# The probabilities' transposes of a two-layer diffusion backbone, moved from a pair of PSUM banks to single banks

## The chip, the core and the metric

The kernel runs on one core of a Trainium2 chip. The core has a matrix engine (PE, whose weight loads are shown apart as PEld), a vector engine (DVE), a scalar engine (ACT), a third elementwise engine (POOL) and a queue that issues DMAs (SP). PE writes its results to PSUM, which this program uses as eight banks of 512 float32 columns on 128 partitions; ACT and DVE read them there. The metric is the device time of one execution in microseconds (us). Lower is better.

## The reference

Two layers run over 128 context tokens and 512 latent tokens of width 1024. Each layer normalises and modulates its input, projects it once, and feeds four parallel mixers: a short gated convolution, windowed attention with eight heads (GQA), neighbourhood attention with four heads (NA) and latent attention with four heads (MLA). The outputs are gated, merged and projected; then comes an MLP. The part that matters here is the softmax attention, which every attention mixer has in this form, cut:

```python
def dense_attention(q, k, v, scale, sink=None):
    ...
    def one_block(qi):
        s = jnp.einsum('nqkgd,nskd->nkgqs', qi, k).astype(jnp.float32) * scale
        p = softmax_sink(s, sink)
        return jnp.einsum('nkgqs,nskd->nqkgd', p.astype(v.dtype), v)
    ...
```

Values are float32. The kernel gets float32 accuracy out of faster matmuls by splitting each operand into a rounded part (hi) and a remainder (lo).

## The kernel before

A layer has three stages: the mixers (`mixers`), the merge of the branches and the MLP. In the merge and the MLP all eight banks are single ones. In the mixers, about 75 to 490 us and 1250 to 1690 us of the span, `psum(4, 2)` cuts them into four single banks (`bank`, tile name pr) and two pairs of two (`banks2`, tile name S2, shown as S). The change touches only the mixers.

There, `attend` goes over 80 blocks of each layer, one block a round: a head has four blocks of 128 latent queries and a short one of 128 context queries. The work of a block is spread over several rounds.

- `block_scores` (lines 503 to 508) takes a pair, computes scores on PE and their minimum on DVE (line 539 with a mask table, line 542 without). `block_exp` (line 548) takes the exponential on ACT from the pair to the tile p in SBUF; it is the last reader of the scores. `block_norm` divides on POOL (line 553). This runs AHEAD = 3 blocks before the block is used.
- `block_T` takes another pair and transposes p on PE, one 128x128 matmul for each chunk of 128 keys (line 562): four, five or six chunks for a latent block, one for a context block. One ACT cast writes the hi part to SBUF (line 566). `block_lo` subtracts it on DVE to get the lo part (line 569); it is the last reader of that pair.
- `pair_pv` (line 579) multiplies two blocks' transposed probabilities by the values into a single bank, read by ACT (line 583) and DVE (lines 592 to 602).
- `fill` puts other matmuls between these steps: the input projection and some of the gates, in halves of 24 matmuls (lines 226 to 228), each half in a single bank that ACT reads afterwards (lines 323, 324, 850, 902), and the small products of MLA (lines 1441 to 1454), whose keys ACT and DVE split (lines 240, 241).

PE's order is the order in which the code calls it. The other engines' orders are set by a scheduler at build time. A tile waits for its bank until the last reader of the tile that held it is done; which of the free banks a tile gets is decided at build time too.

Of the kernel before, what the change touches and what calls it, by code (L numbers as in the profile page):

```python
# [12 lines left out]
ALU = mybir.AluOpType  # L13
# [4 lines left out]
P = 128  # L18
# [58 lines left out]
def _r(ap):  # L77
    return ap.bitcast(F32)


class Net:
# [473 lines left out]
    def block_T(self, B):  # L555
        nc = self.nc
        if B["u"] == 0:
            B["pair"]["pt"] = self.at.tile([P, 2, 6, 256], F32R, name="pt", tag="pt", bufs=2)
        pt, p, nb = B["pair"]["pt"], B["p"], B["nb"]
        tp = self.banks2()  # L560
        for i, s in enumerate(B["pos"]):
            nc.tensor.transpose(tp[:, s * P:(s + 1) * P], p[:, i * P:(i + 1) * P], self.ident)  # L562
        src = tp[:, :nb * P].rearrange("p (c q) -> p c q", q=P)
        qs = slice(B["u"] * P, (B["u"] + 1) * P)
        B["hi"], B["lo"], B["src"] = pt[:, 0, 0:nb, qs], pt[:, 1, 0:nb, qs], src
        nc.scalar.copy(B["hi"], src)  # L566

    def block_lo(self, B):
        self.nc.vector.tensor_tensor(B["lo"], B["src"], _r(B["hi"]), ALU.subtract)  # L569

    def pair_pv(self, R):

# [1050 lines left out]
```

## Time and profile before

| | us |
|---|---|
| median of 3 runs | 2407.87 (2407.02 to 2413.71) |
| the profiled execution | 2411.14 |
| its span, from the first to the last instruction | 2409.3 |
| PE busy in the span | 2319.6 |
| DVE, ACT, POOL busy | 1392.7, 932.9, 415.0 |

An engine that waits shows a gap in the timeline, and the profile names the operation whose end let it go on (`<-`). For PE the table of waits adds such gaps up by its own line and by the releaser. The granted clock (PEclk) is the share of TensorE's full speed that it was given in a stretch; it has the two levels 1.0 (2.4 GHz) and 0.5 (1.2 GHz) here, and a mean between them is a mixture.

### The profile page before, as it was taken

The numbers are of one execution on the slowest core, as the hardware profiler recorded it, in microseconds if no ns is written. First come the engines' busy times: TensorE is split into PE (matmuls) and PEld (weight loads), VectorE is DVE, ScalarE is ACT, GpSimd is POOL, SyncE is SP. The second block draws the span as 40 slices with busy tenths as digits, with TensorE's granted clock in tenths as the row PEclk, the third lists the DMA queues.
The fourth block names the chain that finished last, engine by engine and source line by source line (L and its number), as shares of the span: only waits on it lengthen the run. The fifth ranks groups of instructions, "written<-read, shape, count | busy, mean of one in ns | idle before, by whom it ended". The sixth has DMA issues, their size and how long they took to land. (4 is left out here: it accounts for less than half of the span.)

```text
span 2409.3 us, 39780 instructions
## 1 busy us (share of the span) xinstructions
PE 2319.6 (96%) x15766; PEld 2258.7 (94%) x15766; DVE 1392.7 (58%) x2732; ACT 932.9 (39%) x1891; POOL 415.0 (17%) x496
## 2 busy tenths in 40 slices
PE   8998999899999999999999999999999999999998
PEld 4998889899999999999999999888999999999998
DVE  5765566556775787777576655655434554343433
ACT  5555555442224432322254555553322344231311
POOL 0322233202231000000023233322012300000001
PEclk9999999899999999999999999998999999999999
DMA  6331321154542344444331323220424312222222
GB/s 240 95 103 55 92 89 68 46 202 163 174 155 79 128 153 158 165 142 158 114 133 65 108 96 92 79 71 35 177 92 134 105 45 70 80 71 79 74 84 72
DMA packets 91371, 261.33 MB, mean 108 GB/s; under 512 B 10416, under 2 KB 29232, under 8 KB 89776
## 3 DMA queue, kind: packets, MB, share of 16 engines
q1 hardware_dynamic: 91184, 258.78, 31.8%
q8 instruction: 124, 2.03, 0.3%
q14 instruction: 63, 0.52, 0.1%
HBM read 231.31 MB, written 21.92 MB: 105 GB/s over the span
## 5 line engine op out<-in xcount | busy, mean ns | idle before, releaser
L226 PE MATMUL pr<-hhi,whiw 128*128 128x320 f32 (+1 forms) x2752 | 867.9, 315 | 2.9 <-ACT st L324 1.5
L228 PE MATMUL pr<-hhi,wlow 128*128 128x320 f32 (+1 forms) x2752 | 852.7, 310 | 3.0 <-DVE wlow L193 2.1
L227 PE MATMUL pr<-hlo,whiw 128*128 128x320 f32 (+1 forms) x2752 | 853.3, 310 | 0.0
L226 PEld LDWEIGHTS pr<-hhi,whiw 128*128 128x128 f32 (+1 forms) x2752 | 516.8, 188 | 5.7 <-ACT whiw L192 2.1
L228 PEld LDWEIGHTS pr<-hhi,wlow 128*128 128x128 f32 (+1 forms) x2752 | 515.8, 187 | 5.8 <-DVE wlow L193 3.5
L227 PEld LDWEIGHTS pr<-hlo,whiw 128*128 128x128 f32 (+1 forms) x2752 | 516.8, 188 | 3.6 <-DVE hlo L1249 2.5
L192 ACT CAST whiw<-raww 128x1024 fp32r<-128x1024 f32 (+2 forms) x170 | 173.5, 1021 | 299.8 <-PE pr L227 262.3
L226 PE MATMUL pr<-hh,whiw 128*128 128x320 f32 x832 | 257.1, 309 | 0.0
L228 PE MATMUL pr<-hh,wlow 128*128 128x320 f32 x832 | 256.9, 309 | 0.0
L227 PE MATMUL pr<-hl,whiw 128*128 128x320 f32 x832 | 256.9, 309 | 0.0
L193 DVE TENSOR_TENSOR wlow<-raww,whiw 128x1024 fp32r<-128x1024 f32 (+2 forms) x170 | 208.2, 1225 | 62.1 <-ACT whiw L192 61.6
L1002 DVE SCALAR_TENSOR_TENSOR x<-pr,mod,x 128x256 f32<-128x256 f32 x320 | 107.6, 379 | 188.4 <-PE pr L228 186.2
L1204 POOL TENSOR_TENSOR sqs<-sqs,sq 128x320 f32<-128x320 f32 x48 | 47.7, 993 | 972.1 <-ACT sq L1202 944.4
L553 POOL TENSOR_SCALAR p<-p,sm 128x512 f32<-128x512 f32 (+3 forms) x160 | 118.5, 741 | 440.6 <-DVE sm L552 416.0
L548 ACT ACTIVATE p<-S,sm 128x641 f32<-128x641 f32 (+6 forms) x160 | 111.9, 699 | 181.4 <-DVE sm L539 91.1
L975 POOL TENSOR_TENSOR acc<-acc,sg 128x320 f32<-128x320 f32 x96 | 100.2, 1058 | 340.6 <-DVE sg L974 340.5
L226 PEld LDWEIGHTS pr<-hh,whiw 128*128 128x128 f32 x832 | 156.4, 188 | 0.0
L228 PEld LDWEIGHTS pr<-hh,wlow 128*128 128x128 f32 x832 | 156.4, 188 | 0.0
L227 PEld LDWEIGHTS pr<-hl,whiw 128*128 128x128 f32 x832 | 156.4, 188 | 0.0
L569 DVE TENSOR_TENSOR pt<-S,pt 128x512 fp32r<-128x512 f32 (+3 forms) x160 | 112.1, 701 | 68.7 <-ACT pt L566 67.3
L276 DVE SCALAR_TENSOR_TENSOR junk<-wm,cb 128x1024 bf16<-128x1024 f32 x112 | 136.8, 1222 | 2.0
L190 POOL TENSOR_TENSOR wlow<-raww,whiw 128x512 fp32r<-128x512 f32 (+1 forms) x72 | 92.9, 1290 | 194.8 <-ACT whiw L189 183.1
(224 smaller groups left out, 3820.1 us busy)
## 6 DMA issues: line engine op xcount, KB each, us to landing
raww<-in_w SPq DMA_DIRECT2D x128, 512.0 KB, 3.5
wm<-in_wm SPq DMA_DIRECT2D x80, 512.0 KB, 3.5
raww<-in_wg SPq DMA_DIRECT2D x64, 512.0 KB, 3.7
raww<-in_wa SPq DMA_DIRECT2D x42, 512.0 KB, 3.5
gdram<-gt SPq DMA_DIRECT2D x28, 320.0 KB, 2.2
wm<-in_wm SPq DMA_DIRECT2D x8, 1024.0 KB, 14.5
raww<-in_wo SPq DMA_DIRECT2D x16, 512.0 KB, 3.4
kt<-kt SPq DMA_DIRECT2D x24, 224.0 KB, 4.6
```

Of the source, the lines that this page charges most:

```text
L190: e.tensor_tensor(lo[:, c], raw[:, c], _r(hi[:, c]), ALU.subtract)
L192: nc.scalar.copy(hi, raw)
L193: nc.vector.tensor_tensor(lo, raw, _r(hi), ALU.subtract)
L226: nc.tensor.matmul(out, lhsT=whi[:, kw, :], rhs=xhi[:, kx, sl], start=(i == 0), stop=False)
L227: nc.tensor.matmul(out, lhsT=whi[:, kw, :], rhs=xlo[:, kx, sl], start=False, stop=False)
L228: nc.tensor.matmul(out, lhsT=wlo[:, kw, :], rhs=xhi[:, kx, sl], start=False, stop=(i == n - 1))
L276: nc.vector.scalar_tensor_tensor(self.junk, raw, 1.0, self.cb[v], ALU.mult, ALU.mult, accum_out=self.mod[l]["mod"][:, v, i:i + 1])
L548: nc.scalar.activation(p[:, :B["n"]], B["sc"], AF.Exp, bias=sm[:, 0:1], scale=-1.0, accum_out=sm[:, 1:2])
L553: nc.gpsimd.tensor_scalar(p[:, :n], p[:, :n], sm[:, 1:2], 1.0, ALU.mult, ALU.mult)
L569: self.nc.vector.tensor_tensor(B["lo"], B["src"], _r(B["hi"]), ALU.subtract)
L975: nc.gpsimd.tensor_tensor(a, a, sg, ALU.add)
L1002: self.nc.vector.scalar_tensor_tensor(x[:, j, o + a:o + b], ps[:, a:b], m[:, v, g0 + j:g0 + j + 1], x[:, j, o + a:o + b], ALU.mult, ALU.add)
```

## The change

`block_T` no longer takes a pair. It goes over the chunks four at a time; each group of up to four takes a single bank, and has an ACT cast and a DVE subtraction of its own. A block of one or four chunks has one group as before; the 48 blocks of five chunks are split 4 + 1 and the 32 blocks of six chunks 4 + 2. The two pairs are left to the scores and to the transposes of the values in `v_pair`, three times a layer.

```diff
-        tp = self.banks2()
-        for i, s in enumerate(B["pos"]):
-            nc.tensor.transpose(tp[:, s * P:(s + 1) * P], p[:, i * P:(i + 1) * P], self.ident)
-        src = tp[:, :nb * P].rearrange("p (c q) -> p c q", q=P)
         qs = slice(B["u"] * P, (B["u"] + 1) * P)
-        B["hi"], B["lo"], B["src"] = pt[:, 0, 0:nb, qs], pt[:, 1, 0:nb, qs], src
-        nc.scalar.copy(B["hi"], src)
+        B["split"] = []
+
+        for c0 in range(0, nb, 4):
+            c1 = min(nb, c0 + 4)
+            tp = self.bank()
+            for i, s in enumerate(B["pos"]):
+                if c0 <= s < c1:
+                    nc.tensor.transpose(tp[:, (s - c0) * P:(s - c0 + 1) * P], p[:, i * P:(i + 1) * P], self.ident)
+            src = tp[:, :(c1 - c0) * P].rearrange("p (c q) -> p c q", q=P)
+            B["split"].append((pt[:, 0, c0:c1, qs], pt[:, 1, c0:c1, qs], src))
+            nc.scalar.copy(B["split"][-1][0], src)

     def block_lo(self, B):
-        self.nc.vector.tensor_tensor(B["lo"], B["src"], _r(B["hi"]), ALU.subtract)
+        for hi, lo, src in B["split"]:
+            self.nc.vector.tensor_tensor(lo, src, _r(hi), ALU.subtract)
```

The order of PE's matmuls stays the same, but for the tile that a transpose writes; what moves is what they wait for. The rows below are the built program's, with the other engines on which an instruction waits in brackets. On PE, at a five-chunk block of the first layer's windowed attention, the transposes stand between two pieces of a fill half; before:

```order
L228 MATMUL pr<-hhi,wlow 128x320
L562 MATMUL S_2089<-ident,p 128x128 [waits DVE_49,PE_49,Pool_49]
L562 MATMUL S_2089<-ident,p 128x128 x4
L226 MATMUL pr<-hhi,whiw 128x320
L227 MATMUL pr<-hlo,whiw 128x320
```

and after, with line numbers that are shifted by up to six:

```order
L228 MATMUL pr<-hhi,wlow 128x320
L568 MATMUL pr<-ident,p 128x128 [waits DVE_49,PE_49,Pool_49]
L568 MATMUL pr<-ident,p 128x128 x3
L568 MATMUL pr<-ident,p 128x128 [waits DVE_49,PE_49]
L226 MATMUL pr<-hhi,whiw 128x320
```

The fifth transpose now opens a bank and has a wait of its own. On PE a little later in that round come the scores of the block three ahead; before:

```order
L226 MATMUL pr<-hhi,whiw 128x320
L227 MATMUL pr<-hlo,whiw 128x320
L228 MATMUL pr<-hhi,wlow 128x320
L503 MATMUL S_2111<-kt,qt 128x256 [waits PE_49,Activation_49]
L504 MATMUL S_2111<-kt,qt 128x256
```

and after:

```order
L226 MATMUL pr<-hhi,whiw 128x320 [waits DVE_49,Activation_49]
L227 MATMUL pr<-hlo,whiw 128x320
L228 MATMUL pr<-hhi,wlow 128x320
L503 MATMUL S_2140<-kt,qt 128x256
L504 MATMUL S_2140<-kt,qt 128x256
```

The scores' first matmul no longer waits for ACT there, and the first matmul of a fill half waits for DVE as well as ACT.

On DVE, the third place is the second layer's MLA, where the keys of a head are split while its probabilities are transposed (kt keys, pt transposed probabilities, sm and S2 the minimum of the scores, with buffer numbers); before:

```order
L241 TENSOR_TENSOR qt_16556<-st_16559,qt_16555 96x640
L552 RECIPROCAL sm_16700<-sm_16700 128x1
L190 TENSOR_TENSOR wlow_16748<-raww_16589,whiw_16747 128x512
L241 TENSOR_TENSOR kt_16558<-kr_15925,kt_16557 32x896
L241 TENSOR_TENSOR kt_16558<-pr_16730,kt_16557 64x512
L241 TENSOR_TENSOR kt_16558<-pr_16736,kt_16557 64x384
L193 TENSOR_TENSOR wlob_16744<-rawb_16587,whib_16743 128x384
L542 TENSOR_REDUCE sm_16775<-S2_16768 128x1
L569 TENSOR_TENSOR pt_16719<-S2_16720,pt_16719 128x6x128
```

and after:

```order
L241 TENSOR_TENSOR qt_16748<-st_16751,qt_16747 96x640
L552 RECIPROCAL sm_16897<-sm_16897 128x1
L575 TENSOR_TENSOR pt_16917<-pr_16918,pt_16917 128x4x128
L241 TENSOR_TENSOR kt_16750<-kr_16105,kt_16749 32x896
L241 TENSOR_TENSOR kt_16750<-pr_16930,kt_16749 64x512
L241 TENSOR_TENSOR kt_16750<-pr_16936,kt_16749 64x384
L193 TENSOR_TENSOR wlob_16944<-rawb_16779,whib_16943 128x384
L190 TENSOR_TENSOR wlow_16948<-raww_16781,whiw_16947 128x512
L542 TENSOR_REDUCE sm_16975<-S2_16968 128x1
L575 TENSOR_TENSOR pt_16917<-pr_16924,pt_16917 128x2x128
```

The subtraction of the first four chunks moved ahead of the key splits, and that of a weight (wlow) behind them; the last two chunks stay behind the minimum.

## Rows read from the trace of the kernel before

**Rows 1.** The page: PE's busy time, share and instructions; granted clock in 40 slices.

```profile
PE 2319.6 (96%) x15766; PEld 2258.7 (94%) x15766; DVE 1392.7 (58%) x2732; ACT 932.9 (39%) x1891; POOL 415.0 (17%) x496
...
PEclk9999999899999999999999999998999999999999
```

**Rows 2.** Busy time by stretch, both mixers: length, each engine's us (instructions), clock, DMA.

```profile
75.00:530.00 455.00, 423.90 (x2926) 408.75 (x2924) 270.03 (x588) 228.55 (x523) 127.85 (x172) 0.96 0.28 93
1240.00:1690.00 450.00, 424.72 (x2959) 410.29 (x2958) 273.20 (x586) 231.98 (x542) 133.07 (x174) 0.97 0.26 83
```

**Rows 3.** PE's waits, whole span: us in total, times, longest us.

```profile
PE S L562 <- DVE pt L569: 12.9, 17, 1.6
PE S L503 <- ACT p L548: 12.3, 16, 1.7
...
PE S L506 <- ACT p L548: 7.1, 4, 1.8
...
PE S L503 <- DVE pt L569: 5.2, 3, 2.8
PE S L508 <- DVE kt L241: 4.7, 3, 1.6
PE S L506 <- DVE pt L569: 4.3, 4, 1.1
...
PE S L562 <- ACT p L548: 2.1, 1, 2.1
```

**Rows 4.** Timeline at one wait: start us, us, engine, operation [idle before <-releaser].

```profile
1277.52 0.68 DVE L569 TENSOR_TENSOR pt<-S,pt 128x512 fp32r<-128x512 f32 x1
...
1278.34 0.52 PE L562 MATMUL S<-ident,p 128*128 128x128 f32 x3 [1.62 <-DVE pt L569]
```

**Rows 5.** Groups by shape, ACT's casts and DVE's subtractions: count, busy us, mean ns, idle.

```profile
L566 ACT CAST pt<-S 128x640 fp32r<-128x640 f32 x48 | 33.2, 692 | 16.2 <-PE S L562 16.0
...
L566 ACT CAST pt<-S 128x512 fp32r<-128x512 f32 x48 | 28.1, 586 | 11.2 <-PE S L562 10.6
...
L566 ACT CAST pt<-S 128x128 fp32r<-128x128 f32 x32 | 8.4, 261 | 11.7 <-PE S L562 11.6
...
L569 DVE TENSOR_TENSOR pt<-S,pt 128x640 fp32r<-128x640 f32 x48 | 39.4, 820 | 20.6 <-ACT pt L566 20.2
L569 DVE TENSOR_TENSOR pt<-S,pt 128x512 fp32r<-128x512 f32 x48 | 33.0, 688 | 17.6 <-ACT pt L566 17.1
...
L569 DVE TENSOR_TENSOR pt<-S,pt 128x128 fp32r<-128x128 f32 x32 | 9.1, 286 | 7.0 <-ACT pt L566 6.7
```

**Rows 6.** Ten stretches at the half clock, by stretch: first, last, and their sum.

```profile
191.00:197.80 6.80, 6.24 (x25) 6.20 (x26) 1.76 (x7) 1.81 (x6) 1.06 (x2) 0.50 0.14 51
...
1658.70:1668.90 10.20, 8.32 (x32) 7.36 (x32) 3.85 (x9) 3.42 (x8) 2.71 (x3) 0.50 0.12 46
sum 61.20, PE 52.78 PEld 49.05 DVE 28.45 ACT 20.35 POOL 14.27; mean PE 5.28 PEld 4.91 DVE 2.84 ACT 2.03 POOL 1.43
```

**Rows 7.** Timeline: PE's openings of single banks, and readers that end after them.

```profile
99.82 0.97 PE L579 MATMUL pr<-pt,vt 128*128 128x256 f32 x7
100.10 0.42 ACT L850 COPY st<-pr 128x320 f32<-128x320 f32 x1
...
331.30 0.39 PE L226 MATMUL pr<-hhi,whiw 128*128 128x320 f32 x1
...
332.62 0.44 ACT L902 ACTIVATE gt<-pr 128x320 f32<-128x320 f32 x1
...
381.58 0.85 PE L562 MATMUL S<-ident,p 128*128 128x128 f32 x6
...
383.52 1.15 DVE L241 TENSOR_TENSOR kt<-pr,kt 64x512 fp32r<-64x512 f32 x2
...
1689.29 0.36 PE L226 MATMUL pr<-hhi,whiw 128*128 128x320 f32 x1
...
1690.18 0.42 DVE L602 TENSOR_TENSOR y<-pr,plo 64x256 f32<-64x256 f32 x1
```

## The prediction

> **What bounds the kernel now.** I read the page's busy shares first. PE is busy 96% of the span [rows 1], so time can be won only where PE idles or runs slowly. Next come the busy times of the two stretches that hold the mixers, where alone the change acts: PE is busy 423.9 of 455 us and 424.7 of 450 us, so it idles 31.1 + 25.3 = 56.4 us, at a mean granted clock of 0.96 and 0.97; DVE is busy 59 and 61% there, ACT 50 and 52% [rows 2]. (The first stretch has some 40 us of the merge in it; its PE hardly idles there.) Then the waits of PE, which say whose end let it go on. Six rows have to do with the two pairs: transposes (L562) waiting for the last subtraction (L569) or an exponential (L548), and scores (L503, L506) waiting for an exponential or a subtraction [rows 3]: 12.9 + 12.3 + 7.1 + 5.2 + 4.3 + 2.1 = 43.9 us in 45 waits. That is three quarters of the idle time. The keys of MLA, which DVE splits late (L508 on L241, 4.7 us), are the largest row of another kind in the mixers. The timeline shows what such a wait is: the subtraction of one block's transposes ends at 1278.20, and only then do the next block's transposes start, after 1.62 us of idle PE [rows 4]. Each of the two pairs has in effect one user, so scores wait for the scores of the round before and transposes for the transposes before.
>
> Last, the clock. Ten stretches of the mixers run at 0.50, the lower of the two levels; together they are 61.2 us with PE busy 52.8 us in them [rows 6]. At the upper level that work would take half, so they cost 26.4 us. Most follow a cluster of these waits.
>
> **Removed: the waits on the pairs.** In the new order scores alternate between two pairs, and the first matmul of the scores has no wait for ACT left. A wait ends only when its last condition does, so I looked what is next. For transposes it is POOL's division of p; it had ended before PE arrived at every one of these stalls. For scores it is the queries and keys; where those are late, in MLA, the wait stands in a row of their own already and is not among the six. For the new single banks, the reader of the tile that held the bank before ended after PE's arrival at five stalls, 1.5 us in all. So 43.9 - 1.5 = **42.4 us** go from PE's path. What is late next there is PE's own work.
>
> **Added: waits on the single banks.** Before, four single banks served fill halves and values only. Now 80 + 160 tiles of transposes pass through them too: 555 tiles in place of 315. I paired each tile that opens a single bank in the new program with the tile that held its bank before (the built program names the banks), and took from this trace PE's start of the one and the end of the last reader of the other. The median reserve is 2.75 us, where the same pairing in the old program gives 7.3. In 34 of the 555 the reader ends after PE's start. The first: the values at 99.82 against a copy that ends at 100.52. A fill half at 331.30 would wait for a gate's tanh that ends at 333.06, 1.76 us; six chunks of transposes at 381.58 for the split of keys that ends at 384.67; the last: fill at 1689.29 against 1690.60 [rows 7]. (At 381.58 the wait belongs to the bank of the last two chunks, which PE reaches at 382.04, and to the first half of that split, so it is some 2.2 us.) The 34 come to 34.2 us. Two of them, 7.0 and 3.1 us, rest on a subtraction that stands behind others in DVE's old order; the new order puts it ahead of the key splits, which leaves about 1 us each. And pairs close together share one delay, since PE that waited for the first arrives later at the second. Counted once each, 22 places remain with 18.4 us: the lower bound. The upper one allows for PE arriving earlier by what was just removed, while the late engine does not get faster: if DVE and ACT catch up some 4 us after a wait (they idle 40 to 50%), the sum is about 30 us. I take **24 us**, between these two. On DVE or ACT nothing is queued behind such a wait, since it is PE that waits; behind it on PE stand the rest of the fill half and the next scores.
>
> **Added: work on ACT and DVE.** 48 blocks of five chunks cost 586 + 261 - 692 = 155 ns more on ACT and 688 + 286 - 820 = 154 ns on DVE [rows 5]; with about the same for the 32 blocks of six, 80 x 0.155 = 12.4 us on each, in 905 us in which ACT idles half and DVE 40% [rows 2]. I cost it at nothing, hidden by that idle time. Without this cover it delays a reader by 0.15 us a block, at most where a bank is already late: 34 x 0.15 = 5 us, which the upper bound's surroundings hold.
>
> **The clock.** Two ways to price what returns. In proportion to PE's idle time: 56.4 - 42.4 + 24 = 38.0 us of idle remain, so 26.4 x 38.0 / 56.4 = 17.8 us of the loss remain and 8.6 return. By place: only four of the ten stretches follow waits that stay (keys, a norm's statistics), and if each shrinks to the shortest seen, 3.4 us with a loss of some 1.6, then 6.5 us remain and 19.9 return. New waits are shorter and more scattered than the old ones, so I take the middle, **14 us**.
>
> One rule of the Trainium skill speaks against the change. The page "TensorE: Matmul & The Clock Gate", section "A second HAM failure mode: psum-queue depth-cycling", says that a kernel that cycles through PSUM banks can leave PE idle for moments between its groups of matmuls, often enough that its clock swings between both levels. By that rule more cycling through four banks returns nothing of the 26.4 us, and the sum below would be 18.4 us in place of 32.4. The trace has both sides: clusters of waits with a slow stretch behind them, and single waits such as the 1.62 us of [rows 4] with none.
>
> **The sum.** 42.4 - 24 + 14 = 32.4 us. The profiled execution took 2411.1 us, which gives 2378.7; it lies 3.2 us above the median of the runs, 2407.9, so on the median's footing I predict **2376 us**.
>
> **Rivals.**
> A. The clock does not return: 42.4 - 24 = 18.4 us off, 2389.5. For it: waits at some 22 places remain. The Trainium skill's rule on the clock gate, above, would make this the outcome. Against it: the long stretches, 6.8 and 10.2 us, sit behind clusters of three or four waits, which go.
> B. The waits move and the sum is zero: a wait shows where a late engine meets PE, and DVE and ACT are as late as before. If they need some 15 us to catch up, the same pairing gives 50 us of new waits, more than the 42.4 removed; with 5 to 10 us from the clock this is about 2408. For it: the reserve falls from 7.3 to 2.75 us. Against it: both engines idle 40 to 50%.
> C. Slower: the single banks become the bound. Between the transposes and their subtractions two of four banks are held, one is open for the fill half and one holds the values; a fill half that ends then has no bank to go on in, until DVE has subtracted. The mean of the 34 late pairs is 1.0 us. If each of the 80 split blocks paid it and the slow clock stayed, 80 - 42.4 = 38 us are lost: 2446. It decides from 42 blocks on; the pairing shows 22 places.
> D. The change frees nothing, because scores wait for exponentials that are late whatever the bank. Then only the transposes' 15 us (12.9 + 2.1) go, and 24 come: 9 us slower, 2417. Against it: the exponential is named as the bank's reader, and no data of the scores comes from it.
> E. Full gain: 18.4 us of new waits and 19.9 from the clock, 43.9 off, 2364; with the new waits mostly dodged, 2350.
>
> **How the numbers follow.** My forecast (20 to 43 us off, 2365 to 2388) has 0.50; E 0.10, A (7 to 20 off) 0.20, B 0.12, C and D together 0.08. Two executions of this kernel can be told apart from about 0.3%, 7.2 us, on. Faster by more than that: 0.50 + 0.10 + 0.20 = 0.80; within: 0.12; slower: 0.08. The range leaves out C and D, most of B and the best end of E: 2352 to 2403.
>
> **What would show it.** In the changed kernel's waits of PE, the rows of L503, L506 and of the transposes on L548 and on the subtraction should fall from 43.9 to under 10 us, and rows of the kind "pr L226", "pr L579" (there L585) or the transposes on L902, L241, the additions of the values or the subtraction should appear, 18 to 30 us in all. The ten stretches at half clock should become three to six, of 3.4 us mostly. Idle PE in the mixers should fall from 56 to about 38 us. I am wrong if the new rows sum to over 40 us (B, C), if the scores' rows stay (D), or if the slow stretches keep their 61 us (A).

## The result, and the profile after

The changed kernel takes **2370.91 us** (median of 4 runs, 2370.11 to 2372.24) against 2410.0 us of the kernel before in the same comparison: a ratio of 0.984 with a 95% interval from 0.982 to 0.986. The profiled execution took 2371.4 us, with a span of 2369.6 us; that is 39.7 us less than before.

The first view is the page of the changed kernel: busy time, share and instructions of each engine, and the granted clock in 40 slices.

```profile
PE 2302.6 (97%) x15766; PEld 2245.0 (95%) x15766; DVE 1391.4 (59%) x2812; ACT 935.3 (39%) x1971; POOL 418.9 (18%) x496
...
PEclk9999999999999999999999999999999999999999
```

Beside [rows 1] this splits the 39.7 us in two. PE has the same 15766 matmuls, but is busy 17.0 us less (2319.6 to 2302.6): the same work ran at a higher clock. The rest, 22.7 us, is idle time of PE, which fell from 2409.3 - 2319.6 = 89.7 to 67.0 us.

Next, PE's waits in the changed kernel: line, releaser, us in total, times, longest. The lines have moved by up to six: L568 is the transposes, L571 their cast, L575 their subtraction, L585 the product with the values, L598 and L608 its additions on DVE.

```profile
PE S L508 <- DVE kt L241: 4.0, 3, 1.6
PE pr L568 <- DVE pt L575: 3.5, 6, 1.1
PE pr L226 <- DVE y L598: 3.0, 2, 1.6
...
PE pr L226 <- DVE pt L575: 2.6, 3, 1.9
PE pr L568 <- POOL p L553: 2.6, 3, 1.2
PE pr L585 <- DVE y L608: 1.7, 2, 0.9
PE S L506 <- ACT kt L240: 1.7, 2, 0.8
PE pr L568 <- DVE kt L241: 1.5, 1, 1.5
...
PE S L506 <- ACT p L548: 0.9, 2, 0.5
...
PE S L503 <- ACT p L548: 0.2, 1, 0.2
```

The six rows on the pairs [rows 3] summed to 43.9 us. What is left of them is the last two lines here, 1.1 us. In their place stand some twenty small rows of matmuls that open a single bank ("pr"), most of them of one wait; those that were not there before come to 24.7 us in 30 waits. The largest are shown.

The same two stages as in [rows 2] now look like this (windows: length, busy us of PE, PEld, DVE, ACT and POOL, granted clock, DMA share, GB/s). The first window ends 20 us earlier than in [rows 2] and the second lies 20 us earlier, since the work is done sooner; the second holds 97 matmuls more than in [rows 2], since the work behind the mixers has moved up too.

```profile
75.00:510.00 435.00, 417.09 (x2936) 403.37 (x2935) 269.54 (x632) 230.61 (x565) 129.47 (x172) 0.98 0.30 98
1220.00:1670.00 450.00, 432.73 (x3056) 419.24 (x3055) 281.51 (x639) 240.14 (x592) 135.20 (x174) 0.99 0.29 94
```

PE idles 17.9 + 17.3 = 35.2 us there, where it was 56.4. The stretches of the mixers at the half clock are now six, where [rows 6] had ten:

```profile
187.90:191.30 3.40, 3.40 (x17) 3.36 (x15) 0.57 (x4) 0.41 (x2) 0.90 (x2) 0.50 0.26 100
...
437.10:443.90 6.80, 6.09 (x21) 5.41 (x22) 4.79 (x9) 2.38 (x6) 0.29 (x1) 0.50 0.22 77
...
sum 23.80, PE 23.09 PEld 21.91 DVE 15.91 ACT 7.14 POOL 4.51; mean PE 3.85 PEld 3.65 DVE 2.65 ACT 1.19 POOL 0.75
```

61.2 us of half clock became 23.8.

### The profile page after: what moved, and what is told of

Read it like the earlier page. It is cut to its first block, busy times and chain, and to the rows that moved or that the text cites. A ratio compares the mean times of both kernels' runs of the same rounds, so it can differ in the third digit from the quotient of the medians.

```text
span 2369.6 us, 39989 instructions
## 1 busy us (share of the span) xinstructions
PE 2302.6 (97%) x15766; PEld 2245.0 (95%) x15766; DVE 1391.4 (59%) x2812; ACT 935.3 (39%) x1971; POOL 418.9 (18%) x496
## 5 line engine op out<-in xcount | busy, mean ns | idle before, releaser
L548 ACT ACTIVATE p<-S,sm 128x641 f32<-128x641 f32 (+6 forms) x160 | 112.1, 701 | 156.8 <-DVE sm L539 80.0
L575 DVE TENSOR_TENSOR pt<-pr,pt 128x512 fp32r<-128x512 f32 (+2 forms) x240 | 118.8, 516 | 54.2 <-ACT pt L571 52.9
```

The source lines that it names most:

```text
L548: nc.scalar.activation(p[:, :B["n"]], B["sc"], AF.Exp, bias=sm[:, 0:1], scale=-1.0, accum_out=sm[:, 1:2])
L575: self.nc.vector.tensor_tensor(lo, src, _r(hi), ALU.subtract)
```

## The experiments

The theory: transposes and scores blocked each other through the pairs, and scores needed the second pair; what comes back on the single banks is small because four shared banks leave enough room. The rivals: the gain comes from the finer eviction (two casts and two subtractions, so that the first chunks are free sooner), or from the transposes' waits alone, or the single banks could be had more cheaply. All ratios are to the kernel before, run on the same chip; all edits are to the changed kernel unless another is named. The changed kernel is called "after" here.

### 1. The finer eviction without the banks

```diff
+        tp = self.banks2()
         for c0 in range(0, nb, 4):
             c1 = min(nb, c0 + 4)
-            tp = self.bank()
...
-            src = tp[:, :(c1 - c0) * P].rearrange("p (c q) -> p c q", q=P)
+            src = tp[:, c0 * P:c1 * P].rearrange("p (c q) -> p c q", q=P)
```

> The transposes stay in a pair as in the kernel before; only the casts and subtractions are split at the bank's edge as in the changed kernel (80 more of each). Theory, the banks: the waits on the pairs stay near 44 us, ten or so stretches at half clock stay, time within 6 us of the kernel before (2404 to 2416). Rival, the split itself (a cast can start after four transposes, and the scheduler moves the subtractions forward): half or more of the 39 us gain is here too, 2371 to 2390.

Measured: 2505.62 us, ratio 1.040 (1.038 to 1.042). Neither theory has that. PE's waits of this kernel name the largest part of the reason:

```profile
PE S L568 <- ACT pt L571: 78.3, 80, 3.6
```

In each of the 80 blocks of five or six chunks the second group of transposes waits for the cast of the first group. They lie in two different banks, but in one tile; the timeline shows one such place (start us, us, engine, operation, idle before and its releaser):

```profile
201.22 0.59 ACT L571 CAST pt<-S 128x512 fp32r<-128x512 f32 x1 [1.53 <-PE S L568]
...
201.86 0.33 PE L568 MATMUL S<-ident,p 128*128 128x128 f32 x1 [0.68 <-ACT pt L571]
```

The wait is written into the built program, where the first transpose of a second group waits for ACT:

```
L568 MATMUL S_928<-ident,p 128x128 [waits DVE_49,Pool_49]
L568 MATMUL S_928<-ident,p 128x128 x3
L568 MATMUL S_928<-ident,p 128x128 [waits Activation_49]
```

So it comes from how the program is built, which takes the tile as one thing, and this run says nothing on the question it was made for. It was made again, with all transposes ahead of the first cast.

```diff
+        tp = self.banks2()
+        for i, s in enumerate(B["pos"]):
+            nc.tensor.transpose(tp[:, s * P:(s + 1) * P], p[:, i * P:(i + 1) * P], self.ident)
         for c0 in range(0, nb, 4):
             c1 = min(nb, c0 + 4)
-            tp = self.bank()
-            for i, s in enumerate(B["pos"]):
...
-            src = tp[:, :(c1 - c0) * P].rearrange("p (c q) -> p c q", q=P)
+            src = tp[:, c0 * P:c1 * P].rearrange("p (c q) -> p c q", q=P)
```

> The kernel before with only the evictions split: all transposes of a block go to a pair as before, then two casts and two subtractions, one for each bank, in place of one of each (the first try at this let the fifth and sixth transposes wait for the first cast, 78 us of waits in 80 places, because both groups were in one tile). Theory, the banks: waits on the pairs within 10 us of the 44 of the kernel before, time 2404 to 2420. Rival, the split of the evictions and the new order on DVE bring the gain: 2371 to 2390.

Measured: 2413.36 us in 10 runs, ratio 1.0014 (1.0004 to 1.0023). The waits on the pairs are all there (L565 is the transposes here, L574 the subtraction), 47.1 us in these six rows:

```profile
PE S L565 <- DVE pt L574: 14.9, 19, 1.7
PE S L503 <- ACT p L548: 13.2, 17, 1.7
...
PE S L506 <- ACT p L548: 7.0, 4, 1.8
...
PE S L503 <- DVE pt L574: 4.9, 3, 2.8
...
PE S L506 <- DVE pt L574: 3.7, 4, 1.0
PE S L565 <- ACT p L548: 3.4, 2, 2.1
```

The finer eviction gains nothing; by the interval of the ratio it costs 1 to 6 us where the banks stay as they were. The gain is the banks'.

### 2. Which user of the pairs had to go?

The changed kernel with only one pair, which the scores then have to themselves, and with the two banks of the other pair left empty; and the same with those two banks given to the single ones:

```diff
-            self.ps_stack.enter_context(self.psum(4, 2))
+            self.ps_stack.enter_context(self.psum(4, 1))
```

```diff
-            self.ps_stack.enter_context(self.psum(4, 2))
+            self.ps_stack.enter_context(self.psum(6, 1))
```

> The changed kernel with one pair instead of two for the scores; two banks stay unused, the transposes are in the four single banks as in the changed kernel. Theory, two separate gains: scores that alternate between two pairs are what most of it rests on. Pairing each scores tile with the exponential of the one before in the changed kernel's trace gives 43 late pairs, 58 us raw, 39 us counted once each; with the clock 10 to 15 us more: waits of L503 and L506 on L548 of 25 to 40 us, time 2400 to 2425. Rival, the transposes' leaving is the gain and the scores need one pair only: 2371 to 2382.

> The changed kernel with six single banks and one pair. Pairing: no tile of a single bank is late (median reserve 5.5 us instead of 2.5), scores as with one pair. Theory: the 25 us of waits on single banks go almost all (under 6 us left), the scores' waits of 25 to 40 us come; 12 to 25 us faster than with four single banks and one pair, 2385 to 2405. Rival, the waits on single banks only show that ACT and DVE are late, and move on: no faster than with four single banks and one pair by more than 5 us.

Measured: 2434.09 us (ratio 1.010, 1.009 to 1.012) and 2419.37 us (1.004, 1.003 to 1.006). The two extra banks are worth 14.7 us, as expected, and with them none of the new waits on single banks is left; both times are above their ranges. PE's waits of the first (four singles, one pair):

```profile
PE S L503 <- ACT p L548: 23.6, 21, 2.9
PE S L506 <- ACT p L548: 14.1, 8, 2.0
PE S L503 <- DVE vt L241: 11.5, 5, 3.2
```

and of the second (six singles, one pair):

```profile
PE S L503 <- ACT p L548: 26.7, 23, 2.9
PE S L506 <- ACT p L548: 14.4, 8, 2.0
```

The scores' waits on exponentials come as expected (25 to 40 us): 37.7 us in the first and 41.1 in the second, where [rows 3] have 19.4. Without its stops at the transposes PE reaches the scores sooner and waits there for the same exponentials; the expectation had found these places in the trace of after. Two things come on top. The transposes of the values in `v_pair` also take the pair, and with one pair the scores wait for them, 11.5 us in both kernels; the expectation did not have this wait. And the clock: in the first kernel PE is busy 24.1 us longer than in after (2326.7 against 2302.6), where 10 to 15 us were expected for it.

With the transposes' waits gone and the scores' doubled, 49.2 us of waits on the pair stand in the first kernel where 43.9 had stood, and it is slower than the kernel before. Part of that is the values, which one pair crowds as well and which no run separates. Without their 11.5 us the two kernels would take some 2423 and 2408 us (an estimate: the measured times less this row), still no gain beyond 2 us on the kernel before. So to move the transposes away brings next to nothing by itself; it gains because the scores get two pairs.

### 3. More banks by other cuts

The kernel before with three pairs and two single banks (the cut is the only edit):

```diff
-            self.ps_stack.enter_context(self.psum(4, 2))
+            self.ps_stack.enter_context(self.psum(2, 3))
```

> The kernel before with three pairs and two single banks in the mixers in place of two and four; nothing else changes. The waits on the pairs (44 us) should go, as in the changed kernel. Pairing fill halves and values with the readers of the banks they now get: 72 late, 83 us raw, 54 counted once each. Theory, what counts is that transposes and the rest share four single banks: 5 to 30 us slower than the kernel before, 2413 to 2440. Rival, any third home for the transposes does it: 2371 to 2395.

Measured: 2427.05 us, ratio 1.007 (1.005 to 1.009), as the theory had it. Of the waits on the pairs 9.4 us are left (6.2 in the last row here, 3.2 of transposes that wait for an exponential), where the expectation had none; the others have moved to the singles (L324 reads a half of the projection, L579 is the product with the values):

```profile
PE pr L226 <- ACT st L324: 10.3, 6, 2.9
PE pr L226 <- DVE kt L241: 10.1, 4, 3.2
...
PE pr L579 <- ACT st L324: 6.2, 6, 1.5
PE S L503 <- DVE pt L569: 6.2, 6, 1.8
```

The changed kernel with the four single banks divided: two for the transposes, two for all else (`npr` is 2 in the mixers and all eight elsewhere; lines are shifted by one):

```diff
-        return self.ps1.tile([P, 512], F32, name="pr", tag="pr")
+        return self.ps1.tile([P, 512], F32, name="pr", tag="pr", bufs=self.npr)
...
-            tp = self.bank()
+            tp = self.ps1.tile([P, 512], F32, name="tp", tag="tp", bufs=2)
```

> The changed kernel with two of the four single banks for transposes alone and two for the rest, in place of four for all. Pairing with the changed kernel's trace: 65 late tiles, 74 us raw, 49 counted once each. Theory, sharing is what keeps the new waits at 25 us: 30 to 65 us slower than the changed kernel, 2400 to 2436. Rival, two banks apart serve as well: 2366 to 2380.

Measured: 2420.98 us, ratio 1.005 (1.004 to 1.007), as the theory had it: 50 us more than after, with the same number of banks, instructions and users. Its waits:

```profile
PE pr L227 <- ACT st L325: 11.0, 7, 2.9
PE pr L227 <- DVE kt L242: 9.4, 4, 2.8
PE tp L569 <- DVE pt L576: 9.2, 9, 2.7
...
PE pr L586 <- ACT st L325: 6.1, 6, 1.5
```

This is the shape that the prediction's rival C had described, fill halves that find no bank, and it comes as soon as only two banks serve them. A likely reason, which no run shows by itself: with four that everyone shares, a user who has a late reader borrows from one who has none.

### 4. Can the new waits be made smaller?

The subtraction directly behind the cast, so that the bank comes free sooner (in `attend`, `block_lo` called right behind `block_T`), and ACT copying the whole product with the values to SBUF, so that DVE's additions no longer hold its bank:

```diff
                 self.block_T(B)
+                self.block_lo(B)
...
-            if B:
-                self.block_lo(B)
```

```diff
         nc.scalar.copy(R["plo"][:, :n], ps[64:P, :n])
+        R["phi"] = self.at.tile([64, 256], F32, name="phi", tag="phi", bufs=2)
+        nc.scalar.copy(R["phi"][:, :n], ps[0:64, :n])
...
-        ps, lo, pr = R["ps"], R["plo"], R["pr"]
+        ps, lo, pr = R["phi"], R["plo"], R["pr"]
```

> The changed kernel with the subtraction of the lo part put right behind the transposes in the code, ahead of the scores of the block three ahead, so that the scheduler gives it precedence on DVE and single banks come free sooner. Theory, banks held until the subtraction: the waits on the subtraction (7 us of PE's waits) shrink, 0 to 6 us faster than the changed kernel, 2365 to 2372. Rival, DVE then waits for ACT's cast in front of the scores' minimum: scores' chain late, waits of the transposes on POOL's division grow, 0 to 10 us slower, 2371 to 2381.

> The changed kernel with the values' result copied from its single bank by ACT in whole (two copies of 64 partitions in place of one), so that DVE's addition reads SBUF and the bank is free before it. Theory: the waits of fill and values on those additions (5.9 us in the changed kernel) go, ACT does 96 more copies of 0.26 to 0.37 us beside other work: 0 to 6 us faster, 2365 to 2371. Rival, ACT's casts of the transposes and the exponentials come later and waits on them grow: 0 to 8 us slower, 2371 to 2379.

Measured: 2377.41 us (ratio 0.986, 0.985 to 0.988) and 2376.92 us (0.987, 0.985 to 0.988): about 6 us more than after, which is hardly more than what the intervals can tell apart, and in any case no gain. Both times lie in the ranges of the rivals, but the waits that the rivals named hardly grew: on POOL's division 2.4 us in the first (2.6 in after), of the scores on exponentials 1.8 us in the second (1.1 in after). In the first, PE's waits read (waits between these rows left out):

```profile
PE S L508 <- DVE kt L241: 5.6, 3, 2.4
PE pr L568 <- DVE pt L575: 3.6, 4, 1.4
PE pr L226 <- DVE pt L575: 3.3, 3, 1.9
```

The waits on the subtraction are no smaller (3.5 and 2.6 us in after), and the split of the keys is awaited longer (4.0 in after). In the second, the waits on the additions, 3.0 + 1.7 + 1.2 = 5.9 us in after, were exchanged for waits on the copy that took their place:

```profile
PE pr L226 <- ACT phi L591: 2.6, 3, 1.2
...
PE pr L585 <- ACT phi L591: 2.3, 3, 1.5
```

### 5. Both kernels once more

> The kernel before once more, for its profile: do the ten half-clock stretches of its mixers (61 us) come back in another execution? Theory, the stretches belong to the waits: the waits on the pairs within 3 us of 44 and the stretches within 15 us of 61. Rival, the clock falls partly by chance: waits the same, stretches 30 to 45 us, so that a part of the changed kernel's gain in the profile is luck.

> The changed kernel once more, for its profile. Theory: waits on single banks 22 to 28 us and half-clock stretches of 15 to 35 us in the mixers again, span within 3 us of 2370. Rival, chance: stretches of over 45 us with the same waits.

Measured, in one execution each: 2410.52 us with 45.2 us in the six rows on the pairs and 64.9 us at the half clock in the mixers; 2370.35 us with 1.1 and 20.5 us, and 26.5 us in rows on single banks that the kernel before does not have. The waits and the mixers' slow stretches come back in a second execution of both kernels.

## Why the prediction was right, step by step

**The bound and its place.** PE, in the mixers: 21.2 of the 22.7 us of idle time that went lie in the two stages, and the clock is raised there.

**Waits removed: 42.4 us forecast, 42.8 measured** (43.9 to 1.1). Rival D, that the scores wait for late exponentials whatever the bank, would have left the rows of L503 and L506 on L548; 19.4 us of them became 1.1. Part 2 of the experiments shows the same from the other side: with one pair they are back. (The sum of 43.9 us had left out three waits on the pairs; see the sum below.)

**Waits added: 24 us forecast, 24.7 measured,** in 30 waits where the pairing had 22 places merged and 34 raw. Several stand where it had put them: the values behind a copy, the first place of [rows 7], there 0.70 us late, and the fill half at the end of the second layer's mixers, the last place, there 1.31 us late. The timeline of after at these two:

```profile
100.07 0.43 ACT L856 COPY st<-pr 128x320 f32<-128x320 f32 x1
...
100.55 1.36 PE L585 MATMUL pr<-pt,vt 128*128 128x256 f32 x10 [0.79 <-ACT st L856]
...
1654.71 0.41 PE L226 MATMUL pr<-hhi,whiw 128*128 128x320 f32 x1 [1.22 <-DVE y L608]
```

The transposes that were to wait for the split of keys do so, 1.5 us where the prediction had some 2.2. With each tile followed through the built program into both traces, 16 of the 30 waits (15.1 us) open tiles that the pairing had as late, where the prediction had 18.4 us. The other 14 (9.5 us) open tiles whose bank had come free 0.05 to 5.9 us before PE's start in the old trace. That PE would come sooner was the reason for the upper bound; the 24 us had 5.6 us for it.

Not all of it was right in kind: the fill half that was to wait 1.76 us for a gate's tanh does not wait there, and 2.6 us of the 24.7, three of the 14 waits, are transposes that wait for POOL's division and not for a bank. The prediction had seen that the division ended before PE at every old stall; PE now comes sooner, and at three places it is the division that is late. Two more waits are not for a bank by the built program, 0.8 us for a product of POOL and 0.4 us for a cast. So the match of the sum is in part luck: too much at the late places, too little at the others.

**ACT and DVE: nothing, forecast; no cost of it to be seen.** The price of a split was 155 and 154 ns for a five-chunk block; the means by shape in after give 586 + 271 - 692 = 165 on ACT and 687 + 282 - 820 = 149 on DVE. The busy time rose by less than the 12.4 us of the sum, since the records of a block's two parts overlap: 240 x 516 ns are 123.8 us on DVE, of which 118.8 are busy time. The groups of before and after, with busy us and mean ns:

```profile
L569 DVE TENSOR_TENSOR pt<-S,pt 128x512 fp32r<-128x512 f32 (+3 forms) x160 | 112.1, 701 | 68.7 <-ACT pt L566 67.3
...
L566 ACT CAST pt<-S 128x512 fp32r<-128x512 f32 (+3 forms) x160 | 95.2, 595 | 58.4 <-PE S L562 57.3
```

```profile
L575 DVE TENSOR_TENSOR pt<-pr,pt 128x512 fp32r<-128x512 f32 (+2 forms) x240 | 118.8, 516 | 54.2 <-ACT pt L571 52.9
...
L571 ACT CAST pt<-pr 128x512 fp32r<-128x512 f32 (+2 forms) x240 | 100.8, 454 | 48.7 <-PE pr L568 47.2
```

That is 6.7 us on DVE and 5.6 on ACT, in stages where both idle some 40 to 50%. With the old banks, in the second form of experiment 1, the split cost 1 to 6 us in all; what it costs in after no run shows.

**The clock: 14 us forecast, 17.0 measured over the whole span.** The picture was right (three to six stretches of mostly 3.4 us; six came, five of them of 3.4). In the mixers, where the forecast had put it, half of PE's busy time at the half clock fell from 26.4 to 11.5 us, by 14.8; in the two further executions of experiment 5 it fell by 17.9. So the middle between the two pricings, 8.6 and 19.9, was near, and neither of them alone. The other 2 us or so lie outside the mixers, where the change does nothing: the slow stretches there are 13.9 us before and 10.3 us after, but 6.8 us in both further executions. That part is chance.

The rule of the Trainium skill that spoke against the change (the page "TensorE: Matmul & The Clock Gate", section "A second HAM failure mode: psum-queue depth-cycling"), as the prediction applied it, would have kept the slow stretches: more cycling through banks, more swings of the clock. This trace does not bear that out. Here 555 tiles in place of 315 cycle through the four single banks, and the time at the half clock in the mixers fell from 61.2 to 23.8 us. In this kernel the slow stretches went together with the waits on the pairs; the cycling itself did not bring them on.

**The sum.** By the profile the gain was 39.7 us, not 32.4. Of the difference, 3.0 us are the clock, most of it by chance as just said, and 4.3 us are idle time that 42.4 - 24 = 18.4 did not hold. These are waits that the prediction had left as they were. The keys of MLA [rows 3] fell from 4.7 to 4.0 us, and of these rows of PE's waits before

```profile
PE S L506 <- ACT kt L240: 2.6, 3, 0.9
...
PE pr L226 <- ACT yh L240: 1.2, 2, 0.7
...
PE pr L227 <- DVE yl L241: 0.9, 2, 0.4
...
PE S L562 <- DVE S L532: 0.6, 1, 0.6
PE S L503 <- DVE rta L1316: 0.5, 1, 0.5
PE S L562 <- DVE vt L241: 0.5, 1, 0.5
```

the first is 1.7 us now, and the others are gone: 0.7 + 0.9 + 1.2 + 0.9 + 0.6 + 0.5 + 0.5 = 5.3 us. (A new wait of the scores for keys from a DMA, 0.5 us, goes against them.) The last three should have been in the 43.9 us: in the built program each is the first matmul into a pair, and what it waits for on DVE is the pair's last reader, a subtraction (L569) in the first two and the split of the values in `v_pair` in the third. The profile shows the first two under the name of a neighbour on DVE. These 1.6 us had to go with the change; why PE meets the other late results less often was not tested. The mixers' idle time, forecast at 38.0, is 35.2.

**The rivals.** A (2389.5) fell with the clock. B and C did not come with four shared banks, but what they describe, waits that move to the single banks, came in the cuts with two banks, 2427 and 2421 us. The measured time lies between the forecast and E's 2364. What the prediction did not see is how narrow the place is: of the five new divisions of the banks that were run, the change's and four others, the change's alone is faster than the kernel before.

**Expectations that failed:** the first form of experiment 1, which had a wait of its own; the two absolute times with one pair, where `v_pair` was left out and, in the first, the clock cost 24 us in place of 10 to 15; the faster times of experiment 4, where the new waits were exchanged for others; and the waits on the pairs in the kernel with three pairs, of which 9.4 us stayed.

## What to carry to other kernels

When banks or buffers are dealt out anew, pair each tile of the new program with the last reader of the tile that held its bank, and look both times up in the old trace, with neighbours that share a delay counted once; do the same for the other things that the instruction waits for. A wait that is removed at one place can be met again at the next on the same buffer (19.4 us of the scores' waits became 37.7 with one pair), so ask whether both users get room, not only the one that waits most. Here small tiles with different readers did better in one shared set of four banks than in a set of two for each.

## What the runs showed of the chip that was not expected

**The busy time of PE differs between these kernels almost only by the clock.** For each kernel the table has the idle time of PE over the whole span, the time at the half clock (without the last 6 to 7 us of the span, after PE's last matmul), PE's busy time in it, and PE's busy time less half of that, as if those stretches had run at the upper level (worked out from page and windows).

| kernel | PE idle | half clock | busy in it | PE busy | less half |
|---|---|---|---|---|---|
| before | 89.7 | 75.1 | 66.7 | 2319.6 | 2286.3 |
| after | 67.0 | 34.1 | 33.0 | 2302.6 | 2286.1 |
| finer eviction, old banks | 96.2 | 54.6 | 46.3 | 2313.0 | 2289.8 |
| four singles, one pair | 103.6 | 92.2 | 76.7 | 2326.7 | 2288.3 |
| six singles, one pair | 96.0 | 78.5 | 66.4 | 2317.1 | 2283.9 |
| divided singles | 104.7 | 41.0 | 39.6 | 2312.8 | 2293.0 |

The last column stays within 9 us, while PE's busy time varies by 24. The other kernels lie in the same band, but for the first form of experiment 1 with 2300.3, which was not followed up.

**The slow clock does not follow idle time in proportion.** With divided singles PE idles 104.7 us and has 41.0 us at the half clock; the kernel before idles 89.7 and has 75.1. So it matters where and how PE waits, and a proportional price is not to be trusted in either direction. Which waits bring the clock down is left open: the runs change many waits at once, and none was made to vary one alone. A part differs between executions of one kernel: outside the mixers the kernel before had 13.9 us in one and 6.8 us in the other.

**A tile of two banks is one thing to the built program.** The wait of 78.3 us in the first form of experiment 1 stands between two different banks. That form is 92 us slower than the second one, more than twice what the change gained, and the wait comes from the order in which casts and transposes are written, not from the banks.
